# Moving the SBUF addresses of a matmul's two operands against each other in a single-core encoder layer

## The chip, the cores and the metric

The kernel runs on one core of one Trainium2 chip. The metric is the device time of one execution in microseconds (us). It took 939.85 us, the median of 3 runs (939.79 to 940.05).

## The reference, cut to what matters

One layer of an encoder on 512 tokens of width 1024, all in float32:

```
proj   = rms_norm(x) @ w_in                       # 1024 x 4608: xa, zu, zv, gate_a, gate_b
merged = sig(gate_a) * (s5(xa) @ w_proj_a) + sig(gate_b) * (sgu(zu, zv) @ w_proj_b)
h = x + merged @ w_out
h = h + softmax(q k^T / 16) v @ w_xo              # q from h, k and v from 256 memory rows, 4 heads
h = h + (silu(n @ w_gate) * (n @ w_up)) @ w_down  # n = rms_norm(h), 1024 x 2816 x 1024
out = rms_norm(h)
```

`s5` is a bidirectional state-space scan, `sgu` a gating with a 128x128 position matrix per head.

## The kernel before

**A product in three matmuls.** Every operand of a big product is split in two tiles of type float32r, `hi` (a ScalarE copy, L85) and `lo` (VectorE, source minus hi, L86). `mm3` (L264) and `product` (L1203) then issue three matmuls: hi·hi, hi·lo, lo·hi. TensorE holds one 128x128 piece of an operand, the stationary one, and streams 256 or 512 columns of the other, the moving one. Every matmul loads its own stationary piece, and does so while the matmul before it streams.

**Two shapes.** `feat` and `product` hold the weights and stream the tokens. `tokm` holds the tokens and streams 512 columns of weights. The 512-column products are all of `tokm` and `feat` without `n` or `parts`. The 256-column products are:

- the units of `w_gate` and `w_up` (loop at L1260): 10 units of 7 products of 24 matmuls, in Strassen's manner, on quarters of the tokens. In each unit four products stream quarters of `fn` (960 matmuls in all), and three stream sums of quarters kept in `s1`, `s2`, `s4` (720 matmuls);
- `w_k` on the memory rows `mn` (192), the attention scores with `qq` held and `kt` streamed (96), the first head's `w_q` on halves of `hn` (96), the first columns of `w_gate` on halves of `fn`, half of that with the weights in `s1` and `s2` (96), and the last token block of `w_down` (24).

**Weights.** A plan (`plan_block`, `plan_unit`) lists every block of weights in order of use: a load into `raw` from SP's DMA queue, then the split into one of three `whi` and three `wlo` buffers. Weights run a few blocks ahead of TensorE. The order of instructions on each engine is fixed when the program is built.

**Where the tiles lie.** Pools are laid one behind the other in each partition's memory, in the order in which they are opened, and tiles in a pool by tag, each rounded up to 32 bytes. `const` comes first, then `weights` (raw, hi, lo), `slots` (tags A to E of 16 KB each), `norm`, and then the pool of the stage: `s5`, then `merge`, then `xs` with `attn`, then `xs` with `ffn` and `units`. `const` ends 32 bytes past a multiple of 64, so that the weights and all slots start at remainder 288 by 512, and the small tiles of `norm` leave the stages' pools at remainder 96. All sizes inside are multiples of 512 bytes, so one remainder holds for every slice that a matmul reads. `sums_place` (L110) gives one tile of hi and lo for `s1`, `s2`, `s4`. These hold sums of token quarters in the units, weights of a few blocks at the stages' borders (`place=`), and in `w_down` the activations that `split_act` (L195) makes. `xn`, `hn` and `fn`, the tokens after the three norms, lie with hi in slot B and lo in slot C.

Of the kernel before, what the change touches and what calls it, by code (L numbers as in the profile page):

```python
# [9 lines left out]
F32 = mybir.dt.float32  # L10
F32R = mybir.dt.float32r
# [6 lines left out]
P = 128  # L18
D = 1024
T = 512  # L20
NT = T // P
KD = D // P
# [5 lines left out]
C = 16  # L28
GW = 1024
H = 8  # L30
# [22 lines left out]
def hybrid_layer_kernel(  # L53
# [8 lines left out]
    nc = tc.nc  # L62
# [5 lines left out]
    cp = ctx.enter_context(tc.tile_pool(name="const", bufs=1))  # L68
    wp = ctx.enter_context(tc.tile_pool(name="weights", bufs=3))
    sp = ctx.enter_context(tc.tile_pool(name="slots", bufs=1))  # L70
    np_ = ctx.enter_context(tc.tile_pool(name="norm", bufs=2))
# [11 lines left out]
    def split(dst_hi, dst_lo, src, lo_eng=None):  # L83

        nc.scalar.copy(dst_hi, src)  # L85
        (lo_eng or nc.vector).tensor_tensor(dst_lo, src, dst_hi.bitcast(F32), ALU.subtract)  # L86
# [10 lines left out]
    def halves(src, j=None, place=None):  # L97
        _, k, n = src.shape
        if place is None:
            hi = wp.tile([P, k, n], F32R, tag="hi", name="whi", bufs=3)  # L100
            lo = wp.tile([P, k, n], F32R, tag="lo", name="wlo", bufs=3)
        else:
            hl = sums_place(place, k, n)
            hi, lo = hl[:, 0], hl[:, 1]
        split(hi, lo, src, nc.gpsimd if j is not None and j < 2 else None)
        return hi, lo

    sums_pool = [None]

    def sums_place(i, k, n):  # L110
        return sums_pool[0].tile([P, 2, k, n], F32R, tag=f"s{i}", name=f"s{i}", bufs=1)

    def plan_block(w, kb, k, c0, n, more=None, place=None):
        j, got = len(plan), {}
# [80 lines left out]
    def split_act(kb, kpt):  # L195

        hl = sums_place((1, 2, 4)[kb // kpt % 3], kpt, T)
        split(hl[:, 0], hl[:, 1], acts(kb, kpt))
        for k in range(kpt):
            act_hl[kb + k] = (hl[:, 0, k, :], hl[:, 1, k, :])  # L200
# [57 lines left out]
    def load_raw(j):  # L258
        begin(j, j)
# [121 lines left out]
    make_identity(nc, ident)  # L381
    ones = cp.tile([P, P], F32, name="ones")
    nc.vector.memset(ones, 1.0)
    mhalf = cp.tile([P, 1], F32, name="mhalf")
    nc.vector.memset(mhalf, -0.5)

    def sum_sq(dst, src):
# [36 lines left out]
    xsp = [None]  # L424
# [6 lines left out]
    def slot(tag, shape, dt, name):  # L431
        return sp.tile(list(shape), dt, tag=tag, name=name)


    s5 = ExitStack()
    s5p = s5.enter_context(tc.tile_pool(name="s5", bufs=1))
# [9 lines left out]
    for t in range(NT):  # L446
# [4 lines left out]
            load_raw(0)  # L451
        elif t < 3:
            load_raw(t)
    xn_hi = slot("B", (P, KD, T), F32R, "xn_hi")
    xn_lo = slot("C", (P, KD, T), F32R, "xn_lo")
    xn = (xn_hi, xn_lo)
    for t in range(NT):
        rms_scale(xt[:, t, :], g_mix, xt[:, t, :])
# [402 lines left out]
        nc.scalar.activation(z, z, AF.Copy, scale=r)  # L861

    nc.sync.dma_start(wsr, sgu_w[0].rearrange("h t s -> t h s"))
    gbr = np_.tile([2 * H, P], F32, tag="gbr", name="gbr", bufs=1)
    nc.sync.dma_start(gbr[0:H, :], sgu_ln_g[0].rearrange("(h d) -> h d", d=P))
    nc.sync.dma_start(gbr[H:2 * H, :], sgu_ln_b[0].rearrange("(h d) -> h d", d=P))
    mix = np_.tile([P, H, P], F32, tag="gain", name="mix", bufs=2)
# [75 lines left out]
    s5.close()  # L943
    mgx = ExitStack()
    mgp = mgx.enter_context(tc.tile_pool(name="merge", bufs=1))


    yg_hi = mgp.tile([P, 4, T], F32R, name="yg_hi")
# [37 lines left out]

    at = ExitStack()
    xsp[0] = ctx.enter_context(tc.tile_pool(name="xs", bufs=2))
    ap_ = at.enter_context(tc.tile_pool(name="attn", bufs=1))

    h = slot("A", (P, NT, D), F32, "h")
    for t in range(NT):
        nc.sync.dma_start(h[:, t, :], x[t * P:(t + 1) * P, :])
    hn_hi = slot("B", (P, KD, T), F32R, "hn_hi")
    hn_lo = slot("C", (P, KD, T), F32R, "hn_lo")
    hn = (hn_hi, hn_lo)

    mn_hi = ap_.tile([P, KD, M], F32R, tag="mq", name="mn_hi", bufs=2)
# [36 lines left out]


    mn = (mn_hi, mn_lo)
    kt_hi = ap_.tile([P, KD, M], F32R, name="kt_hi")
    kt_lo = ap_.tile([P, KD, M], F32R, name="kt_lo")
    vt_hi = ap_.tile([P, NM, D], F32R, name="vt_hi")  # L1040
# [79 lines left out]

    g_f = gain(ffn_norm_g[0], "g_f")
    ot = (ot_hi, ot_lo)
    fn_hi = slot("B", (P, KD, T), F32R, "fn_hi")
    fn_lo = slot("C", (P, KD, T), F32R, "fn_lo")
    fn = (fn_hi, fn_lo)

    tokm(w_xo, 0, ot, KD, add_evac(0, 1, None), hook=lambda: values(XH - 1, *pts.pop()))
# [52 lines left out]
    a11, a12, a21, a22 = full[:, K0, T0], full[:, K1, T0], full[:, K0, T1], full[:, K1, T1]  # L1180

    def make_op(q, i, src):
        hl = sums_place(i, 4, 256)
        ops[q] = (hl[:, 0], hl[:, 1])
        split(*ops[q], src)

    def sum1():
        V.tensor_tensor(a22, a21, a22, ALU.subtract)
        make_op(5, 1, a22)

    def sum2():
        V.tensor_tensor(s3, a11, a21, ALU.subtract)
        V.tensor_tensor(a11, a22, a11, ALU.subtract)
        make_op(6, 2, a11)

    def sum4():
        V.tensor_tensor(a12, a12, a11, ALU.add)
        make_op(3, 4, a12)
# [176 lines left out]
```

## Time and profile before

| | |
|---|---|
| Median of the runs | 939.85 us |
| The profiled execution, its own time | 940.4 us |
| Its span, first to last instruction | 938.6 us |
| Granted TensorE clock, mean | 0.997 |
| VectorE busy | 577.9 us (62%) |
| ScalarE busy | 442.2 us (47%) |
| GpSimd busy | 84.9 us (9%) |

The chain of work that ended last runs 86% of the span on TensorE. A matmul's duration in the profile is from its start to the modelled end of its last column, so that neighbours overlap. What tells the pace is the distance from one matmul's start to the next one's; a view in order of time gives the starts. "x2" in such a row stands for two equal instructions one behind the other.

### The profile page before, as it was taken

How to read it: one execution, taken by the hardware profiler on the slowest of the kernel's cores; microseconds unless marked ns; L12 is line 12 of the kernel's file. 1: busy time of each engine (PE TensorE's matmuls, PEld its weight loads, DVE VectorE, ACT ScalarE, POOL GpSimd, SP SyncE). 2: the span in 40 equal slices, each digit the busy share in tenths (PEclk: the TensorE clock that was granted, in tenths of full speed). 3: DMA queues.
4: the chain of work that ended last, by engine and by line, in shares of the span. 5: the costliest groups of instructions: out<-in, count | busy, mean ns of one | idle time of the engine just before them, and what ended most of it. 6: DMA issues, size and time to landing. Idle time of an engine off the chain costs nothing.

```text
span 938.6 us, 14044 instructions
## 1 busy us (share of the span) xinstructions
PE 922.0 (98%) x5579; PEld 808.0 (86%) x5579; DVE 577.9 (62%) x943; ACT 442.2 (47%) x643; POOL 84.9 (9%) x136
## 2 busy tenths in 40 slices
PE   7999999999999999999999999999999999999997
PEld 6878888888888888789888888999999999888785
DVE  5696653898462167667545455867667777545544
ACT  5532984244554343545444344644545445433433
POOL 3004210000052104110000001000000000000000
PEclk9999999999999999999999999999999999999999
DMA  8445223323243363735522156244545651222212
GB/s 282 136 135 148 66 91 100 114 90 108 72 115 100 90 204 110 246 91 184 186 80 68 46 174 163 68 112 121 150 116 143 137 122 46 90 90 90 90 67 90
DMA packets 93249, 111.04 MB, mean 118 GB/s; under 512 B 12144, under 2 KB 72064, under 8 KB 93184
## 3 DMA queue, kind: packets, MB, share of 16 engines
q1 hardware_dynamic: 82688, 99.95, 34.4%
q0 software_dynamic: 7328, 7.84, 5.0%
q10 hardware_dynamic: 3168, 2.36, 0.8%
q8 instruction: 44, 0.72, 0.3%
q14 instruction: 21, 0.17, 0.0%
HBM read 103.34 MB, written 6.78 MB: 117 GB/s over the span
## 4 chain that ended last, share of the span: by engine, by line
PE 86%; ACT 5%; DVE 4%; DMA 3%; issue 2%; POOL 1%; SPq 0%; POOLq 0%; DVEq 0%; ACTq 0%
PE pf L267 31%; PE pt L267 24%; PE px L1212 12%; PE pq L1212 6%; PE pv L1212 3%; PE pk L662 1%; DMA b<-in_w_gate_dram 1%; PE po L267 1%; PE psc L267 1%; DMA wraw<-in_w_in_dram 1%; ACT whi L85 1%; PE ptr L419 1%; DVE wlo L86 1%; PE psv L910 1%; PE py L770 1%
## 5 line engine op out<-in xcount | busy, mean ns | idle before, releaser
L86 DVE TENSOR_TENSOR wlo<-wraw,whi 128x1024 fp32r<-128x1024 f32 x110 | 136.9, 1246 | 122.6 <-ACT whi L85 115.2
L85 ACT CAST whi<-wraw 128x1024 fp32r<-128x1024 f32 x112 | 117.6, 1051 | 146.5 <-PE pf L267 82.9
L267 PE MATMUL pt<-whi,s 128*128 128x512 f32 x344 | 107.3, 394 | 1.0 <-ACT whi L85 1.0
L267 PE MATMUL pf<-xn_lo,whi 128*128 128x512 f32 x224 | 88.0, 393 | 0.0
L267 PE MATMUL pf<-xn_hi,whi 128*128 128x512 f32 x224 | 87.9, 393 | 0.0
L267 PE MATMUL pf<-xn_hi,wlo 128*128 128x512 f32 x224 | 87.6, 391 | 0.0
L267 PEld LDWEIGHTS pt<-whi,s 128*128 128x128 f32 x344 | 64.3, 187 | 17.0 <-ACT whi L85 1.2
L86 DVE TENSOR_TENSOR wlo<-b,whi 128x1024 fp32r<-128x1024 f32 x40 | 49.0, 1224 | 36.7 <-ACT whi L85 36.7
L85 ACT CAST whi<-b 128x1024 fp32r<-128x1024 f32 x40 | 42.0, 1051 | 62.3 <-PE px L1212 28.6
L1212 PE MATMUL px<-fn_hi,whi 128*128 128x256 f32 x240 | 68.0, 283 | 1.5 <-ACT u L1270 1.5
L1212 PE MATMUL px<-fn_lo,whi 128*128 128x256 f32 x240 | 68.0, 283 | 0.0
L1212 PE MATMUL px<-fn_hi,wlo 128*128 128x256 f32 x240 | 67.9, 283 | 0.0
L267 PE MATMUL pt<-wlo,s 128*128 128x512 f32 x172 | 67.0, 394 | 0.0
L1212 PE MATMUL pq<-s,whi 128*128 128x256 f32 x320 | 57.1, 280 | 0.0
L86 DVE TENSOR_TENSOR s<-a,s 128x1024 fp32r<-128x1024 f32 x22 | 26.9, 1225 | 48.6 <-ACT s L85 48.6
L267 PEld LDWEIGHTS pf<-xn_hi,whi 128*128 128x128 f32 x224 | 42.1, 188 | 8.8 <-issue 0.2
L267 PEld LDWEIGHTS pf<-xn_hi,wlo 128*128 128x128 f32 x224 | 42.1, 188 | 8.6
L267 PEld LDWEIGHTS pf<-xn_lo,whi 128*128 128x128 f32 x224 | 42.1, 188 | 8.4
L1212 PEld LDWEIGHTS pq<-s,whi 128*128 128x128 f32 x320 | 49.1, 188 | 0.2
L85 ACT CAST s<-a 128x1024 fp32r<-128x1024 f32 x22 | 23.0, 1047 | 54.7 <-PE pt L267 54.7
L86 DVE TENSOR_TENSOR wlo<-t,whi 128x1024 fp32r<-128x1024 f32 x30 | 36.7, 1224 | 18.5 <-ACT whi L85 18.5
L1212 PEld LDWEIGHTS px<-fn_hi,whi 128*128 128x128 f32 x240 | 46.0, 192 | 1.8 <-ACT u L1270 1.8
(352 smaller groups left out, 2316.6 us busy)
## 6 DMA issues: line engine op xcount, KB each, us to landing
wraw<-in_w_in_dram SPq DMA_DIRECT2D x36, 512.0 KB, 3.8
wraw<-in_w_down_dram SPq DMA_DIRECT2D x22, 512.0 KB, 3.6
b<-in_w_gate_dram SPq DMA_DIRECT2D x15, 512.0 KB, 3.9
b<-in_w_up_dram SPq DMA_DIRECT2D x15, 512.0 KB, 4.2
wraw<-in_w_proj_b_dram SPq DMA_DIRECT2D x8, 512.0 KB, 3.7
wraw<-in_w_out_dram SPq DMA_DIRECT2D x8, 512.0 KB, 4.4
wraw<-in_w_k_dram SPq DMA_DIRECT2D x8, 512.0 KB, 4.6
wraw<-in_w_v_dram SPq DMA_DIRECT2D x8, 512.0 KB, 3.6
```

The costliest lines, as they stand in the source:

```text
L85: nc.scalar.copy(dst_hi, src)
L86: (lo_eng or nc.vector).tensor_tensor(dst_lo, src, dst_hi.bitcast(F32), ALU.subtract)
L267: nc.tensor.matmul(ps, a[x], b[y], start=start and i == 0, stop=stop and i == 2, skip_group_check=free)
L419: nc.tensor.transpose(ps[:, j, :], src[:, k * P:(k + 1) * P], ident)
L662: nc.tensor.matmul(ps[32 * j:32 * j + 32, q, :], bd[i][:, g].rearrange("p d c -> p (d c)"), lc(es[i], g), start=(i == 0), stop=False, tile ...
L770: nc.tensor.matmul(ps[:, g, :], tt[:, g, :], u[:, o * GO + g, :], start=True, stop=False)
L910: nc.tensor.matmul(ps[:, t * P:(t + 1) * P], zt[:, t, h * P:(h + 1) * P], wst[:, h, :], start=True, stop=True)
L1212: nc.tensor.matmul(ps[:, j, :], a[x], b[y], start=start and j == k == i == 0, stop=k == 3 and i == 2, skip_group_check=True)
```

## The change

It changes addresses. What each engine computes stays: the instructions of TensorE, ScalarE and VectorE are the same in the same order. Three small clears on GpSimd are new, and two loads stand elsewhere in SP's queue.

- `mhalf` takes 36 bytes instead of 4, which moves all that lies behind it by 32.
- `xn`, `hn` and `fn` become one tile of hi and lo in tag B, with 512 bytes to spare; `fn` starts 64 bytes in. Tag C goes.
- `sums_place` has 512 bytes to spare too, and an argument `shift`: the sums of token quarters start 320 bytes in; weights and activations placed there start at 0.
- Pads of 192 bytes at the start of `merge` and of `xs`, and one of 64 bytes, `shift`, ahead of `kt` and `vt`; each is cleared once.
- `gbr`, which had a tag of its own, takes a buffer of tag "gain".

Start addresses by 512, in the built programs (the difference is moving minus stationary, by 512):

| products | moving, stationary before | difference | after | difference |
|---|---|---|---|---|
| 512 columns, weights with xn, hn, yb, mg, ot | 288, 288 | 0 | 320, 320 | 0 |
| 512 columns, `w_down` and `w_v` | 288, 96 | 192 | 320, 320 | 0 |
| 512 columns, yg, ya, part of `w_xo` | 96, 288 | 320 | 320, 320 | 0 |
| 512 columns, first `w_up` block on fn | 288, 288 | 0 | 384, 320 | 64 |
| 512 columns, attention values | 96, 96 | 0 | 384, 384 | 0 |
| 256 columns, units on fn | 288, 288 | 0 | 384, 320 | 64 |
| 256 columns, units on sums | 96, 288 | 320 | 128, 320 | 320 |
| 256 columns, scores | 96, 96 | 0 | 384, 320 | 64 |
| 256 columns, `w_k` on mn | 96, 288 | 320 | 320, 320 | 0 |
| 256 columns, first head's `w_q` | 288, 288 | 0 | 320, 320 | 0 |
| 256 columns, fn with weights in s1, s2 | 288, 96 | 192 | 384, 320 | 64 |
| 256 columns, last block of `w_down` | 288, 96 | 192 | 320, 320 | 0 |

All starts before are 32 past a multiple of 64; all starts after are multiples of 64.

```diff
-    def sums_place(i, k, n):
-        return sums_pool[0].tile([P, 2, k, n], F32R, tag=f"s{i}", name=f"s{i}", bufs=1)
+    def sums_place(i, k, n, shift=0):
+        t = sums_pool[0].tile([P, 2 * k * n + 128], F32R, tag=f"s{i}", name=f"s{i}", bufs=1)
+        return t[:, shift:shift + 2 * k * n].rearrange("p (h k n) -> p h k n", h=2, k=k)
+
+    def align(pool):
+
+        pad = pool.tile([P, 48], F32, name="pad", bufs=1)
+        nc.gpsimd.memset(pad, 0.0)
...
-    mhalf = cp.tile([P, 1], F32, name="mhalf")
+    mhalf = cp.tile([P, 9], F32, name="mhalf")[:, 0:1]
...
+    def token_slot(name, shift=0):
+
+        t = sp.tile([P, 2 * KD * T + 128], F32R, tag="B", name=name)
+        hl = t[:, shift:shift + 2 * KD * T].rearrange("p (h k t) -> p h k t", h=2, k=KD)
+        return hl[:, 0], hl[:, 1]
...
-    xn_hi = slot("B", (P, KD, T), F32R, "xn_hi")
-    xn_lo = slot("C", (P, KD, T), F32R, "xn_lo")
+    xn_hi, xn_lo = token_slot("xn")
...
-    gbr = np_.tile([2 * H, P], F32, tag="gbr", name="gbr", bufs=1)
+    gbr = np_.tile([2 * H, P], F32, tag="gain", name="gbr", bufs=2)
...
     mgp = mgx.enter_context(tc.tile_pool(name="merge", bufs=1))
+    align(mgp)
...
     xsp[0] = ctx.enter_context(tc.tile_pool(name="xs", bufs=2))
+    align(xsp[0])
...
-    hn_hi = slot("B", (P, KD, T), F32R, "hn_hi")
-    hn_lo = slot("C", (P, KD, T), F32R, "hn_lo")
+    hn_hi, hn_lo = token_slot("hn")
...
+    shift = ap_.tile([P, 16], F32, name="shift")
+    nc.gpsimd.memset(shift, 0.0)
     kt_hi = ap_.tile([P, KD, M], F32R, name="kt_hi")
...
-    fn_hi = slot("B", (P, KD, T), F32R, "fn_hi")
-    fn_lo = slot("C", (P, KD, T), F32R, "fn_lo")
+    fn_hi, fn_lo = token_slot("fn", 16)
...
-        hl = sums_place(i, 4, 256)
+        hl = sums_place(i, 4, 256, 80)
```

## The prediction

> **What bounds the kernel now.** I first read the page's busy times and its granted clock.
>
> ```profile
> PE 922.0 (98%) x5579; PEld 808.0 (86%) x5579; DVE 577.9 (62%) x943; ACT 442.2 (47%) x643; POOL 84.9 (9%) x136
> PEclk9999999999999999999999999999999999999999
> ```
>
> TensorE is never long without a matmul and its clock is full. Then busy times by stage (columns: window, length, busy and instruction count of PE, PEld, DVE, ACT, POOL, then clock, DMA share, GB/s):
>
> ```profile
> 90.00:175.00 85.00, 84.00 (x496) 72.64 (x495) 49.22 (x108) 58.81 (x88) 10.29 (x21) 1.00 0.31 97
> 580.00:810.00 230.00, 227.34 (x1852) 224.22 (x1852) 167.43 (x169) 116.80 (x147) 11.37 (x10) 1.00 0.44 109
> 810.00:932.00 122.00, 121.72 (x536) 97.91 (x535) 59.81 (x66) 46.99 (x59) 1.66 (x3) 1.00 0.25 86
> ```
>
> In the units VectorE, the next busiest, works 167.4 of 230 us. So the time is the number of matmuls times their spacing, and the change can act only through the spacing. The view in order of time gives it: the first and the last start of a stretch, divided by the matmuls from one to the other. Here are five address cases: fn in a unit, a sum in a unit, xn, `w_down`, yg; and below them `w_k` and the program's last matmuls.
>
> ```profile
> 637.05 0.29 PE L1212 MATMUL px<-fn_hi,wlo 128*128 128x256 f32 x1
> ...
> 639.93 0.28 PE L1212 MATMUL px<-fn_hi,wlo 128*128 128x256 f32 x1
> ```
> ```profile
> 634.21 0.28 PE L1212 MATMUL px<-s,wlo 128*128 128x256 f32 x1
> ...
> 636.33 0.28 PE L1212 MATMUL px<-s,wlo 128*128 128x256 f32 x1
> ```
> ```profile
> 180.10 0.39 PE L267 MATMUL pf<-xn_hi,whi 128*128 128x512 f32 x1
> ...
> 186.90 0.39 PE L267 MATMUL pf<-xn_hi,whi 128*128 128x512 f32 x1
> ```
> ```profile
> 816.36 0.39 PE L267 MATMUL pt<-wlo,s 128*128 128x512 f32 x1
> ...
> 824.76 0.39 PE L267 MATMUL pt<-wlo,s 128*128 128x512 f32 x1
> ```
> ```profile
> 340.45 0.39 PE L267 MATMUL pf<-yg_hi,whi 128*128 128x512 f32 x1
> ...
> 346.63 0.39 PE L267 MATMUL pf<-yg_hi,whi 128*128 128x512 f32 x1
> ```
> ```profile
> 426.04 0.28 PE L267 MATMUL pf<-mn_hi,wlo 128*128 128x256 f32 x1
> ...
> 427.06 0.28 PE L267 MATMUL pf<-mn_hi,wlo 128*128 128x256 f32 x1
> ```
> ```profile
> 929.29 0.28 PE L267 MATMUL pcut<-wlo,s 128*128 128x256 f32 x1
> ...
> 931.34 0.28 PE L267 MATMUL pcut<-wlo,s 128*128 128x256 f32 x1
> ```
>
> The same element comes back every third matmul, so the counts are multiples of three. Spacing: fn 2.88 us / 24 = 120.0 ns; sums 2.12 / 18 = 117.8; xn 6.80 / 30 = 226.7; `w_down` 8.40 / 36 = 233.3; yg 6.18 / 27 = 228.9; `w_k` here 1.02 / 9 = 113.3; the last ones 2.05 / 18 = 113.9.
>
> Two things are to be seen. **Equal work has unequal spacing by address**: 512 columns take 226.7 ns at difference 0, 228.9 at 320, 233.3 at 192. And **the spacings come in steps**: 256 more columns at difference 0 cost 226.7 - 120.0 = 106.7 ns for 1024 bytes, while 120.0 - 113.3 and 233.3 - 226.7 are both 6.67 ns, a sixteenth of 106.7. So a step is 64 bytes of the moving operand, and in steps the spacings are 17, 17 2/3 and 18 for 256 columns, whose data fill 16, and 34, 34 1/3 and 35 for 512 columns, whose data fill 32. Nothing falls below 17. I read that as reads in 64-byte blocks: 1024 bytes that start 32 past a multiple of 64 touch 17 blocks, 2048 touch 33, and the rest (nothing to two steps) is lost to the weight load beside them, by the difference of the addresses.
>
> **The change part by part.** TensorE, VectorE and ScalarE issue the same instructions, so the sum has one kind of term: a class's matmuls times its change of spacing. Counts are from the loops.
>
> *All starts become multiples of 64.* If the first step is the straddled block, each of the 4620 float32r matmuls loses 6.67 ns: 30.8 us. The trace of before shows no float32r operand at a multiple of 64, so this is bounded: nothing, if the seventeenth step is a fixed gap between matmuls, or one step. I take one step, as 113.3 is the floor in two classes and is exactly 17 blocks.
>
> *Differences.* Where rows show a case, I keep what it loses beyond the first step: one step at 0, and 2/3 of a step at 320 with 256 columns. A difference of 64 isn't shown; its nearest row is 320 with sums, the other odd number of blocks near it: 2/3 of a step, 111.1 ns when aligned. Bounds: no loss (106.7) and two steps as in `w_down` (120.0).
>
> | class | matmuls | before, ns | after, ns | us |
> |---|---|---|---|---|
> | fn in units, scores | 1056 | 120.0 | 111.1 | -9.4 |
> | sums in units | 720 | 117.8 | 111.1 | -4.8 |
> | 512 columns at 0, stays | 1536 | 226.7 | 220.0 | -10.2 |
> | `w_down`, `w_v`: 192 to 0 | 612 | 233.3 | 220.0 | -8.2 |
> | yg, ya, `w_xo`: 320 to 0 | 192 | 228.9 | 220.0 | -1.7 |
> | first head's `w_q` | 96 | 120.0 | 113.3 | -0.6 |
> | `w_k`, fn with s1/s2, last block, `w_up`'s first, values | 408 | | | -1.7 |
>
> The last row is a rest of small classes, estimated from the same steps. Sum: -36.6 us.
>
> A rule of the Trainium skill ("TensorE: Matmul & The Clock Gate", section "Back-to-back issue gap") gives a warm spacing of columns / 2.4 + 2.5 ns, so 109.2 and 215.8 here. The rows lie above it throughout, 113.3 at the least. If all classes came down to it, the estimated sum would be -52 us and the time 888.
>
> *What doesn't become time.* Up to 175 us VectorE feeds the scan and the order is fixed, so a faster TensorE meets some waits earlier. About 480 float32r matmuls lie there, 3.2 us by one step; I count half, +1.6. Later VectorE has room: 167.4 us in a units stage that shrinks from 230 to about 215.
>
> *The rest of the edits.* Three clears of 192 bytes or less on GpSimd and a moved `g_mem` load:
>
> ```profile
> 358.73 3.52 POOL L979 TENSOR_TENSOR mg<-mg,part 128x512 f32<-128x512 f32 x2 [50.21 <-issue]
> ```
> ```profile
> 141.01 8.46 SPq L118 DMA_DIRECT2D wraw<-in_w_in_dram  x2
> 151.66 9.26 SPq L895 DMA_DIRECT2D gad<-gas  x2
> ```
> ```profile
> 148.21 0.23 PE L877 MATMUL pgb<-ident,gbr 16*128 16x16 f32 x1
> ```
>
> GpSimd idles 50 us before the merge's first addition, which covers the first pad; without that cover it would cost a fraction of a microsecond there. `g_mem` now shares `gbr`'s buffer, so its load stands in SP's queue between the two weight loads of the 141 us row and waits for the transpose at 148.2. The second of them is issued by 149.5 at the latest (the row's end), so one SP issue may slip by about 1 us, with weights running two blocks ahead: nothing. `mix` waits for the last read of `g_mix` early on: nothing. Uncovered, both together would cost 1 to 2 us.
>
> Sum: 940.4 - 36.6 + 1.6 = 905.4 for the profiled execution; it ran 0.55 over the median, so **905 us**.
>
> **The rivals.**
>
> *Alignment does nothing, differences do* (the seventeenth step is a fixed gap). For: no row shows an aligned operand. Against: a fixed gap needn't be exactly one block long. Then fn and scores gain 2.2 ns x 1056 = 2.3 us, `w_down` and `w_v` 6.67 x 612 = 4.1, yg 0.4; `w_k` goes from 320 to 0 and loses about 0.6, small classes 0.4. Net -5.8: 934.
>
> *Alignment helps one of the shapes alone*, because with 256 columns the weight load fills nearly the whole spacing (PEld 224.2 of 230 us in the units) and with 512 it doesn't (97.9 of 122). Only 512 columns: -20.6 - 1.7 = -22; only 256: -16 - 4.5 = -20. About 919.
>
> *Slower.* At difference 64 the moving operand runs one block ahead of the weights, as `w_down`'s runs three ahead at 192, and loses a step more than level instead of a third less: 126.7 ns on 1056 matmuls, +7.0 us. Without an alignment gain, `w_down` gives back 4.1 and `w_k` and small ones take 0.7: 943 or so. It decides if 64 costs more than 124 ns in the units. Against: sums at 320 and `w_k` are below level.
>
> *Nothing changes.* The spacing could hang on what is held and streamed and not on addresses: `w_down` streams weights, the units stream tokens. Then 940. Against it are the two spacings of `feat` alone, 226.7 on xn and 228.9 on yg, and the 120.0 and 117.8 of one line, L1212. The Trainium skill ("SBUF — State Buffer", section "Who interferes with whom") says that TensorE reads the moving operand and the weights through two independent ports and never waits for anyone, by which no address could matter; these four rows disagree.
>
> **How the numbers follow.** Forecast 0.50; differences alone 0.24; one shape alone 0.13; slower 0.08; nothing 0.05. The forecast's own range is 897 to 913: half a step more or less on the 2340 matmuls of 512 columns in the table is 7.8 us. The range that leaves out no more than 2 in 10 must take in one shape alone and differences alone with fn at its bounds: 898 to 937. Faster by over 0.2% (about what a measurement of this kernel can tell from no change) 0.87, within 0.05, slower 0.08.
>
> **What would show it.** In the profile after: xn's spacing 220 against 226.7 decides on alignment; `w_down` must equal xn (if it stays at 233, the address difference isn't its cause); fn in the units at 111 and sums at 111 as well; `w_k` no more than 113.3. Busy VectorE and ScalarE stay at 578 and 442 us. A wait on `wraw` near 150 us, or a longer gap in TensorE before 175 us, would show the cost of what I left at nothing. It is wrong if xn stays at 226.7, or if fn rises above 120.

## The result and the profile after

The changed kernel took 929.79 us (median of 6 runs, 928.02 to 935.31) against 939.84 for the kernel before on the same chip: a ratio of 0.989, 95% interval [0.9857, 0.9923]. The forecast was 905 us. The sign was right, the size less than a third of what was said. Two later series of the changed kernel gave 931.07 us (0.9906, [0.9879, 0.9932]) and 935.68 us (0.9937, [0.9912, 0.9962]). Why one kernel has these medians is a part of the answer below.

The profiled execution after took 929.58 us, with a span of 927.8. The page's busy times and granted clock:

```profile
PE 910.8 (98%) x5579; PEld 801.7 (86%) x5579; DVE 577.3 (62%) x943; ACT 442.3 (48%) x643; POOL 85.0 (9%) x139
PEclk9999999999999999999999999999999999999999
```

TensorE still bounds the kernel, with the same 5579 matmuls; VectorE and ScalarE are busy as before. So the difference lies in the spacing, and the view in order of time gives it again: fn in a unit, sums in a unit, xn, `w_down`, `w_k` (line numbers have moved: L1225 is `product`, L273 `mm3`).

```profile
637.17 0.28 PE L1225 MATMUL px<-fn,wlo 128*128 128x256 f32 x1
...
639.89 0.28 PE L1225 MATMUL px<-fn,wlo 128*128 128x256 f32 x1
```
```profile
628.78 0.39 PE L1225 MATMUL pq<-s,whi 128*128 128x256 f32 x2
...
631.16 0.39 PE L1225 MATMUL pq<-s,whi 128*128 128x256 f32 x2
```
```profile
179.99 0.39 PE L273 MATMUL pf<-xn,wlo 128*128 128x512 f32 x1
...
186.79 0.39 PE L273 MATMUL pf<-xn,wlo 128*128 128x512 f32 x1
```
```profile
816.10 0.39 PE L273 MATMUL pt<-wlo,s 128*128 128x512 f32 x1
...
824.26 0.39 PE L273 MATMUL pt<-wlo,s 128*128 128x512 f32 x1
```
```profile
428.14 0.28 PE L273 MATMUL pf<-mn_hi,wlo 128*128 128x256 f32 x1
...
430.30 0.28 PE L273 MATMUL pf<-mn_hi,wlo 128*128 128x256 f32 x1
```

Spacing: fn 2.72 us / 24 = 113.3 ns (before 120.0); sums 2.38 / 21 = 113.3 (117.8); xn 6.80 / 30 = 226.7 (226.7); `w_down` 8.16 / 36 = 226.7 (233.3); `w_k` 2.16 / 18 = 120.0 (before 113.3 in part and 117.8 in the rest). The decisive row is xn: every start is a multiple of 64 now, and not a nanosecond has gone.

By stages: from the first unit's product on sums to the first `w_down` matmul took 191.50 us before and 182.62 after, from there to the start of the last matmul 128.81 and 125.66. Up to the units the changed kernel is 1.32 us later. That sums to -10.7; the spans differ by 10.8. The 1.32 come from a stretch at half clock, which cost 1.6 us, less 0.3 won on the way, and not from an edit. Windows before, then after (length, busy of PE, PEld, DVE, ACT, POOL, granted clock, DMA share, GB/s):

```profile
10.00:15.00 5.00, 3.58 (x10) 2.49 (x11) 3.96 (x5) 4.14 (x11) 4.20 (x3) 0.66 1.04 346
30.00:40.00 10.00, 10.00 (x52) 7.98 (x50) 5.63 (x18) 6.62 (x9) 0.00 (x0) 1.00 0.46 123
```
```profile
10.00:15.00 5.00, 2.65 (x11) 1.73 (x11) 4.06 (x5) 4.50 (x12) 4.20 (x3) 1.00 1.03 339
30.00:40.00 10.00, 10.00 (x45) 7.86 (x44) 5.03 (x16) 6.01 (x8) 0.00 (x0) 0.83 0.34 100
```

Both executions lose 1.7 us' worth of clock, (1 - 0.66) x 5 and (1 - 0.83) x 10: once while TensorE waits for the first loads (busy 3.58 of 5 us), where it costs nothing, and once under full work, where it costs 1.6 us. The Trainium skill ("TensorE: Matmul & The Clock Gate", section "What's actually happening") says that the clock is set by a free-running window of about 3.4 us, so that the place of a change varies from run to run; with that these rows agree. The Trainium skill there puts half clock behind an idle window, which they don't show: in the changed kernel TensorE is busy for all of the 4 us from 30 to 34, and the clock is half from 34 on.

### The profile page after: what moved, and what is told of

The parts are those of the page before. It is cut to its first block, busy times and chain, and to the rows that moved or that the text cites. A ratio compares the mean times of both kernels' runs of the same rounds, so it can differ in the third digit from the quotient of the medians.

```text
span 927.8 us, 14051 instructions
## 1 busy us (share of the span) xinstructions
PE 910.8 (98%) x5579; PEld 801.7 (86%) x5579; DVE 577.3 (62%) x943; ACT 442.3 (48%) x643; POOL 85.0 (9%) x139
## 4 chain that ended last, share of the span: by engine, by line
PE 85%; ACT 5%; DVE 4%; DMA 3%; issue 2%; POOL 1%; SPq 0%; POOLq 0%; ACTq 0%; DVEq 0%
PE pf L273 31%; PE pt L273 24%; PE px L1225 11%; PE pq L1225 6%; PE pv L1225 3%; PE pk L673 1%; DMA b<-in_w_gate_dram 1%; PE po L273 1%; ACT whi L85 1%; PE psc L273 1%; DVE wlo L86 1%; DMA wraw<-in_w_in_dram 1%; PE ptr L425 1%; PE psv L921 1%; PE py L781 1%
## 5 line engine op out<-in xcount | busy, mean ns | idle before, releaser
L273 PE MATMUL pf<-xn,whi 128*128 128x512 f32 x448 | 141.0, 393 | 0.0
L273 PE MATMUL pt<-whi,s 128*128 128x512 f32 x344 | 105.4, 390 | 1.0 <-ACT whi L85 1.0
L273 PEld LDWEIGHTS pf<-xn,whi 128*128 128x128 f32 x448 | 83.7, 188 | 17.2 <-issue 0.2
L273 PE MATMUL pf<-xn,wlo 128*128 128x512 f32 x224 | 87.6, 391 | 0.0
L1225 PE MATMUL px<-fn,whi 128*128 128x256 f32 x480 | 83.9, 277 | 1.6 <-ACT u L1283 1.6
L273 PEld LDWEIGHTS pt<-whi,s 128*128 128x128 f32 x344 | 64.5, 188 | 14.7 <-ACT whi L85 1.2
L1225 PEld LDWEIGHTS px<-fn,whi 128*128 128x128 f32 x480 | 72.6, 188 | 1.8 <-ACT u L1283 1.7
L1225 PE MATMUL px<-fn,wlo 128*128 128x256 f32 x240 | 66.4, 277 | 0.0
L273 PE MATMUL pt<-wlo,s 128*128 128x512 f32 x172 | 66.2, 390 | 0.0
L1225 PE MATMUL pq<-s,whi 128*128 128x256 f32 x320 | 55.1, 276 | 0.0
L273 PEld LDWEIGHTS pf<-xn,wlo 128*128 128x128 f32 x224 | 42.1, 188 | 8.5
L1225 PEld LDWEIGHTS pq<-s,whi 128*128 128x128 f32 x320 | 48.3, 188 | 0.2
L85 ACT CAST whi<-t 128x1024 fp32r<-128x1024 f32 x30 | 31.6, 1054 | 31.9 <-PE pv L1225 11.3
L273 PE MATMUL pt<-whi,xn 128*128 128x512 f32 x128 | 43.3, 411 | 2.0 <-ACT xn L85 1.7
L1225 PEld LDWEIGHTS px<-fn,wlo 128*128 128x128 f32 x240 | 45.1, 188 | 0.0
```

The source lines that it names most:

```text
L273: nc.tensor.matmul(ps, a[x], b[y], start=start and i == 0, stop=stop and i == 2, skip_group_check=free)
L1225: nc.tensor.matmul(ps[:, j, :], a[x], b[y], start=start and j == k == i == 0, stop=k == 3 and i == 2, skip_group_check=True)
```

## The experiments

Theory first: only the difference of the two addresses counts. Rival: the forecast's blocks, where alignment takes a step off each matmul.

**e1_off64**: the changed kernel with everything 32 past a multiple of 64 again, same differences.

```diff
-    mhalf = cp.tile([P, 9], F32, name="mhalf")[:, 0:1]
+    mhalf = cp.tile([P, 1], F32, name="mhalf")
```

> The changed kernel with mhalf back at 4 bytes: every address behind it moves by 32, so all starts are 32 past a multiple of 64 again and every difference stays that of the changed kernel. Theory D (differences alone count): as the changed kernel, 929.8 us, units at 113.3 ns on fn and on sums. Theory A (the sums came down from 117.8 to 113.3 because of the multiples of 64): units at 117.8 ns throughout, 4.5 ns x 1680 = 7.5 us more, 937.

Measured 935.47 us (927.16 to 940.13, 9 runs), 0.9913 [0.9878, 0.9948]; the profiled execution 927.16. xn and fn in its view in order of time:

```profile
179.88 0.39 PE L273 MATMUL pf<-xn,wlo 128*128 128x512 f32 x1
...
182.60 0.39 PE L273 MATMUL pf<-xn,wlo 128*128 128x512 f32 x1
...
641.54 0.28 PE L1225 MATMUL pv<-fn,wlo 128*128 128x256 f32 x1
...
642.22 0.28 PE L1225 MATMUL pv<-fn,wlo 128*128 128x256 f32 x1
```

2.72 / 12 = 226.7 and 0.68 / 6 = 113.3: as aligned. Its nine runs lie at 927.2 to 927.4 (four) and 935.5 to 940.1 (five); of that below. Its half-clock stretch lay where that of before lies, and its span is 925.4, 13.2 below before, where the 10.8 of the changed kernel and the 1.6 us that the stretch didn't cost here make 12.4.

**e2_align**: the kernel before, aligned, all differences kept (the diff of e1_off64 turned round).

> The kernel before with mhalf at 36 bytes: all starts multiples of 64, every difference as before. Theory D: as before, 939.8 us, fn 120.0, sums 117.8, w_down 233.3 ns. Theory A: sums at 113.3 ns, 4.4 x 720 = 3.2 us less, 936.6.

Measured 940.65 us, 0.9997 [0.9984, 1.001].

```profile
180.27 0.39 PE L267 MATMUL pf<-xn_hi,wlo 128*128 128x512 f32 x1
...
182.31 0.39 PE L267 MATMUL pf<-xn_hi,wlo 128*128 128x512 f32 x1
...
636.89 0.28 PE L1212 MATMUL px<-fn_hi,wlo 128*128 128x256 f32 x1
...
638.33 0.28 PE L1212 MATMUL px<-fn_hi,wlo 128*128 128x256 f32 x1
```

2.04 / 9 = 226.7 and 1.44 / 12 = 120.0. Alignment to 64 does nothing, alone or with the rest.

**e3_fn**: of the change, only fn at 64; sums stay at 320, `w_down` at 192.

```diff
-    fn_hi = slot("B", (P, KD, T), F32R, "fn_hi")
-    fn_lo = slot("C", (P, KD, T), F32R, "fn_lo")
+    fn_hi, fn_lo = token_slot("fn", 16)
```

(`xn`, `hn` by `token_slot` too, unshifted, and `gbr` in tag "gain", for the room.)

> The kernel before with fn alone moved by 64 bytes (xn, hn, fn in one tile, gbr in tag gain, nothing else): in the units fn at difference 64, sums still at 320, all 32 past a multiple of 64. Theory D with history (a product at 0 puts the next ones at 113.3's slower neighbour 117.8, products at 64 and 320 hold 113.3): both at 113.3, 6.4 + 3.2 = 9.6 us less, 930. Theory A: fn and sums 117.8, 2.1 us less, 937.7.

Measured 931.44 us (930.93 to 933.66), 0.9904 [0.9888, 0.992]. The sums, whose addresses it doesn't touch:

```profile
628.31 0.39 PE L1216 MATMUL pq<-s,whi 128*128 128x256 f32 x2
...
630.69 0.39 PE L1216 MATMUL pq<-s,whi 128*128 128x256 f32 x2
```

2.38 / 21 = 113.3 in place of 117.8. So a product's pace is not its own alone: the products before it seem to count. This is one profile, and the pace turns out below to vary by execution; but all five runs lie within 3 us, and no run of the kernel before comes down to where sums at 113.3 would put it.

**e4_down**: only `w_down`'s operands level, in the kernel before.

```diff
-    def sums_place(i, k, n):
+    def sums_place(i, k, n, shift=48):
...
-        hl = sums_place(i, 4, 256)
+        hl = sums_place(i, 4, 256, 0)
```

> The kernel before with weights and activations in s1, s2, s4 moved level with the other weights, sums where they were: w_down from difference 192 to 0. Both theories: w_down 226.7 instead of 233.3 ns, 3.4 us less, and 0.3 us back in the first columns of w_gate; 936.7. If w_down stays at 233.3 it is its roles and not its addresses.

Measured 938.85 us, 0.997 [0.9957, 0.9982].

```profile
820.13 0.39 PE L268 MATMUL pt<-wlo,s 128*128 128x512 f32 x1
...
822.85 0.39 PE L268 MATMUL pt<-wlo,s 128*128 128x512 f32 x1
```

2.72 / 12 = 226.7: this part of the change is worth what it says, 3 us.

**f1_128, f2_192, f3_256, f4_32**: fn, sums, xn and hn moved together to another distance from the weights, in search of a pace below the floor. The edit, with n = 32, 48, 64 elements of four bytes:

```diff
-    xn_hi, xn_lo = token_slot("xn")
+    xn_hi, xn_lo = token_slot("xn", n)
...
-    hn_hi, hn_lo = token_slot("hn")
+    hn_hi, hn_lo = token_slot("hn", n)
...
-    fn_hi, fn_lo = token_slot("fn", 16)
+    fn_hi, fn_lo = token_slot("fn", n)
...
-        hl = sums_place(i, 4, 256, 80)
+        hl = sums_place(i, 4, 256, n)
```

(f4_32: 8 for fn and sums, 4 for xn and hn.)

> The changed kernel with fn, the sums, xn and hn all 128 bytes past the weights' remainder. So far 256 columns took 120.0 ns at differences 0 and 256, and 113.3 or 117.8 at 64, 192 and 320. Theory P (an odd number of 64-byte blocks between the two streams is good, an even one is bad): 256 columns 120.0 ns, as level; about 940 us. Theory N (only nearness to level or to 256 is bad): 113.3 or 117.8. For 512 columns on xn, P gives 226.7 as at 0.

> The same with 192 bytes. Theory P: units at 113.3 ns as with 64 and 320, 226.7 there no more: 512 columns on xn at 228.9 (as 64 and 320, tokens streamed) to 233.3 (192 in w_down, weights streamed), about 5 us more than the changed kernel, 935. If 64 and 320 are special, the units stay at 117.8 or above.

> The same with 256 bytes. Theory P and the 120.0 ns seen on fn at 256 with weights in s1 and s2: units at 120.0, xn at 226.7 as level; about 940 us.

> The changed kernel with fn and the sums 32 bytes past the weights' remainder, xn and hn 16 bytes past. If blocks of 64 bytes count, 32 and 16 bytes are still the same block for half the stream or more: 117.8 to 120.0 ns for 256 columns, 226.7 for 512. If a smaller block counts, 32 bytes are one block or more and the units come to 113.3, or under it.

One run each: 941.78, 933.79, 938.41, 937.38 us. xn in f1_128, f2_192 and f3_256:

```profile
180.33 0.39 PE L273 MATMUL pf<-xn,wlo 128*128 128x512 f32 x1
...
182.42 0.40 PE L273 MATMUL pf<-xn,wlo 128*128 128x512 f32 x1
```
```profile
180.66 0.39 PE L273 MATMUL pf<-xn,wlo 128*128 128x512 f32 x1
...
183.46 0.39 PE L273 MATMUL pf<-xn,wlo 128*128 128x512 f32 x1
```
```profile
180.01 0.39 PE L273 MATMUL pf<-xn,wlo 128*128 128x512 f32 x1
...
182.05 0.39 PE L273 MATMUL pf<-xn,wlo 128*128 128x512 f32 x1
```

2.09 / 9 = 232.2; 2.80 / 12 = 233.3; 2.04 / 9 = 226.7. With the units' spacings, over all traces:

| difference by 256 | 512 columns, ns | 256 columns, ns |
|---|---|---|
| 0 | 226.7 | 120.0 |
| 16 | 231.7 | 119 |
| 32 | 233 | 117 |
| 64 | 229 | 113.3 or 117.8 |
| 128 | 232 | 119 to 120 |
| 192 | 233.3 | 113.3, at places 117.8 |

256 is like 0, and 320 like 64: so far as these two pairs show it, the period is 256 bytes. The figures are those of settled stretches: the attention values, level in every version but in runs of a dozen matmuls at most, took 230 to 231 ns. The two widths want opposite things, level for 512 and not level for 256. Nothing fell below 113.3 and 226.7.

**g3_cut and h1_cut64: what the floor is.** Every level 512-column matmul of some stages is cut in two over the same weights.

```diff
+        c = width[0] if ps.shape[-1] == 512 else None
         for i, (x, y) in enumerate(((0, 0), (0, 1), (1, 0))):
+            if c:
+                nc.tensor.matmul(ps[:, :c], a[x], b[y][:, :c], start=start and i == 0, stop=stop and i == 2, skip_group_check=True)
+                nc.tensor.matmul(ps[:, c:], a[x], b[y][:, c:], start=False, stop=stop and i == 2, skip_group_check=True)
+                continue
```

> The changed kernel with every 512-column matmul on the stages' normed tokens, attention and w_down cut in two over the same weights, all level: 384 and 128 columns on xn and yb, 320 and 192 on hn and mn, 256 and 256 on ot and in w_down. Theory of a fixed gap: a level matmul takes its columns at 106.67 ns per 256 and 13.33 ns beside them (120.0 and 226.7 fit that), so 384 columns take 173.3, 320 take 146.7, 128 take 66.7 if no weight load holds them, 256 take 120.0; about 2000 cuts cost 13.3 ns each, 27 us, some 956 us. Rival: the columns themselves go one seventeenth slower than 16 columns in 6.67 ns, and what lies above is the difference's: then 384 take 170.0, 320 take 141.7, and only the halves of w_down and ot cost 13 ns (the level 120.0), 9 us, some 939. A weight load longer than a short piece would show as a pace above both for 128 and 192 columns.

> The changed kernel with 512-column matmuls cut in two over the same weights, level, at other widths: 448 and 64 columns on xn and yb, 352 and 160 on hn and mn; ot, w_down and the first w_up block stay whole. The cuts of 384 and 128 took 286.7 ns a pair, 60.0 over the whole, and those of 320 and 192 took 257.5; a fixed gap alone says 240. Theory of a floor: a matmul's columns take 106.67 ns per 256 and 13.3 beside them, but no matmul is shorter than the load of the weights that follow it, about 113.3. Then 448 and 64 take 186.7 + 13.3 + 113.3 = 313.3 a pair, 352 and 160 take 146.7 + 13.3 + 113.3 = 273.3. Rival: the dearer pairs come from the cut itself (the same weights loaded twice, the second piece's start within the row), not from the short piece's length; then a pair costs 286.7 or 257.5 at these widths too. Units, with the first w_up block whole, at 113.3 by the theory that this block sets their pace; at 117.8 if it was anything else in the cuts of before.

Measured 1015.83 and 1060.3 us, one run each. The first is far above both expectations, 956 and 939; the theory of a floor was made from its spacings, and h1_cut64 tests it at other widths. (h1_cut64's granted clock was 0.76 from 20 to 120 us; its spacings are taken from behind that.) Pairs of 384 and 128 on xn in g3_cut; of 448 and 64 on xn, and 352 and 160 on hn, in h1_cut64:

```profile
181.32 0.39 PE L277 MATMUL pf<-xn,wlo 128*128 128x384 f32 x1
181.54 0.22 PE L278 MATMUL pf<-xn,wlo 128*128 128x128 f32 x1
...
183.90 0.39 PE L277 MATMUL pf<-xn,wlo 128*128 128x384 f32 x1
```
```profile
300.38 0.45 PE L277 MATMUL pf<-xn,wlo 128*128 128x448 f32 x1
300.67 0.19 PE L278 MATMUL pf<-xn,wlo 128*128 128x64 f32 x1
...
302.26 0.45 PE L277 MATMUL pf<-xn,wlo 128*128 128x448 f32 x1
...
624.44 0.36 PE L277 MATMUL pf<-hn,wlo 128*128 128x352 f32 x1
...
627.68 0.36 PE L277 MATMUL pf<-hn,wlo 128*128 128x352 f32 x1
```

A pair takes 2.58 / 9 = 286.7, 1.88 / 6 = 313.3 and 3.24 / 12 = 270.0 ns; 320 and 192 took 257.5 in g3_cut, and two level halves of 256 took 2 x 120.0. A fixed gap says 240 for all of them, a gap in proportion to the columns 227, a price of the cut itself one number for all. Columns at 106.7 per 256, 13.3 beside them, and **no matmul that takes less than some 110 to 113 ns** say 283 to 287, 310 to 313, 270 to 273 and 257 to 260. (So taken, 128 and 64 columns came out at 113.3, 192 at 110.8 and 160 at 110.0.) Only whole pairs can be read so: inside a pair the starts lie 0.22 and 0.06 us apart, so the wait shows behind the long piece's start. The rows of the weight loads (PEld) of g3_cut tell why a pair is long:

```profile
181.26 0.19 PEld L277 LDWEIGHTS pf<-xn,wlo 128*128 128x128 f32 x1
181.37 0.19 PEld L278 LDWEIGHTS pf<-xn,wlo 128*128 128x128 f32 x1
181.55 0.19 PEld L277 LDWEIGHTS pf<-xn,whi 128*128 128x128 f32 x1
```

The load for a long piece starts when the short one before it starts (181.54 and 181.55), and the next load comes 0.11 us behind it; over all the cut stages of both kernels, never less than 107 ns behind. The kernel before has the floor too, without a cut, in matmuls of the scan and of the gating on plain float32:

```profile
140.06 1.89 PE L719 MATMUL pz<-u,wt 128*128 128x64 f32 x16
169.81 1.84 PE L910 MATMUL psv<-wsx,zt 128*128 128x128 f32 x15
```

But for the first one, the starts of both lie 111 to 112 ns apart, with 64 columns as with 128, and every one loads 128x128 weights. So 113.3 is the least that a 256-column matmul with a new 128x128 load took: a floor that doesn't go with the columns, and no block. That it is the load itself fits all these rows, but no run changed the load. The Trainium skill ("TensorE: Matmul & The Clock Gate", section "LDWEIGHTS (loading the stationary operand)") gives a load of 128 columns 128 / 1.2 = 107 ns; the 0.11 us from load to load agree, and the floor of the spacing is 3 to 7 ns above that.

**g1_sums0, c_after, h2_up256: the two paces.** g1_sums0 puts the sums level, fn stays at 64; h2_up256 cuts the first `w_up` block in halves (`width[0] = 256` around that one `feat`); c_after is the changed kernel again.

```diff
-        hl = sums_place(i, 4, 256, 80)
+        hl = sums_place(i, 4, 256)
```

> The changed kernel with the sums of token quarters placed level with the weights (difference 0), fn still at 64. Theory of two paces: at differences 64 and 320 a 256-column product runs at 113.3 or at 117.8 ns, whichever the matmuls before it left behind, and a level product between them leaves 117.8. Then fn in the units runs at 117.8 here and the sums at 120.0; against the changed kernel that is 960 x 4.4 ns + 720 x 6.7 ns = 9 us more, some 938 us. Rival: each product has the pace of its own difference and 64 has 113.3. Then fn stays at 113.3, the sums go to 120.0, and it is 4.8 us more, some 934.

> The changed kernel with one edit: the first w_up block on fn (48 matmuls of 512 columns at difference 64) is cut in halves of 256 columns. Theory that the pace is left behind by the matmuls before: the 256-column products ahead of it run at 117.8 and nothing of 512 columns comes between, so the whole units, 1680 matmuls with unchanged addresses and unchanged instructions, run at 117.8 in place of 113.3: 7.5 us more, some 938 us. Rival: the units' pace comes from their own addresses; then they stay at 113.3 and the time within 0.5 us of the changed kernel's.

> The changed kernel once more, on the same chip as the others of this call, for the comparison: some 930 us against 940 by every theory.

Measured 936.29 (one run), 942.15 (one run, at half clock from 580 to 587 us) and 931.07 us (927.52 to 936.51). In g1_sums0 fn ran at 117.8 and the sums at 120.0, in h2_up256 everything in the units ran at 117.8, both as the theory of paces said. But so did the units in c_after's profiled execution (935.3 us), where nothing was changed: its units took 189.55 us against 182.62. So h2_up256 shows nothing of its own, and g1_sums0 only that level sums take 120.0. And in h1_cut64, where the `w_up` block was whole, they ran at 117.8: that this block sets the pace has fallen.

**g2_best, k_192, c_after2.** g2_best: fn and sums at 192, and mn at 64. k_192: fn and sums at 192 alone. c_after2: the changed kernel a third time, beside k_192.

```diff
-    fn_hi, fn_lo = token_slot("fn", 16)
+    fn_hi, fn_lo = token_slot("fn", 48)
...
-        hl = sums_place(i, 4, 256, 80)
+        hl = sums_place(i, 4, 256, 48)
```

> The changed kernel with fn and the sums at 192 in place of 64 and 320, and mn at 64 (one more pad of 64 bytes ahead of it, which puts w_v's operands 64 the other way). Theory of two paces: at 192 the 256-column products ran at 113.3 all the way, so the 195 that run at 117.8 in the changed kernel gain 0.9 us, the first w_up block loses 48 x 4.5 ns = 0.2, w_k goes from 120.0 to 113.3 or 117.8 and gains 0.4 to 1.3 us, w_v stays or gains 0.1: 1.1 to 2.1 us below the changed kernel, some 928. Rival: the pace of 192 hung on xn and hn being at 192 too; then it is level with the changed kernel or a little above.

> The changed kernel with fn and the sums at 192 in place of 64 and 320, and nothing else. At 64 and 320 the units ran at 113.3 ns in the first profile of the changed kernel and at 117.8 in the second, 7.5 us apart over 1680 matmuls, and its times fall in two groups, 928 to 931 and 935 to 937. Theory that 192 fixes the pace: at 192 the units ran at 113.3 in both profiles there are, so the median is some 929 (0.9 us for the products ahead of the units, which run at 117.8 at 64, less 0.2 us for the first w_up block) and no run lies above 933. Rival: 192 has both paces too, by execution; then some third of the runs lie at 935 to 938 here as well.

> The changed kernel a third time, on the chip of the run beside it, for the count of the two groups: by the theory of a pace chosen anew in each execution, some runs at 927 to 931 and some, a third or so, at 935 to 937; by the rival that the second profile was a disturbance, all at 927 to 931.

g2_best: 929.92 us (927.86 to 932.83), 0.9876 [0.9856, 0.9896], not told apart from c_after beside it. mn at 64 gave `w_k` 117.8, but `w_v`, 64 the other way, 233.3 in place of 226.7, a loss where none was expected. k_192: 928.50 us (927.60 to 929.44), 0.9869 [0.9852, 0.9885], the fastest version and the steadiest; c_after2 935.68 (927.58 to 936.86). fn in a unit of c_after2 and of k_192:

```profile
641.65 0.28 PE L1225 MATMUL px<-fn,wlo 128*128 128x256 f32 x1
...
643.77 0.28 PE L1225 MATMUL px<-fn,wlo 128*128 128x256 f32 x1
```
```profile
637.26 0.28 PE L1225 MATMUL px<-fn,wlo 128*128 128x256 f32 x1
...
639.98 0.28 PE L1225 MATMUL px<-fn,wlo 128*128 128x256 f32 x1
```

2.12 / 18 = 117.8 and 2.72 / 24 = 113.3. The changed kernel's 19 runs in the three series fall in two groups, ten from 927.5 to 931.5 and nine from 934.3 to 936.9; the profiled ones show why: the units take 182.6 or 189.6 us, by execution.

## Why the prediction was wrong

**The step that failed** is "All starts become multiples of 64": "I take one step, as 113.3 is the floor in two classes and is exactly 17 blocks." Nothing was to be had; this step carried 30.8 of the 36.6 us. Two facts had been put into one: 113.3 at 256 columns is the floor of a matmul with a new load, and 226.7 at 512, level, is 32 steps of columns and 13.3 ns beside them. That both are multiples of 17 is chance by this reading. The level rows shown before the result already held the other reading, 120.0 = 106.7 + 13.3 and 226.7 = 213.3 + 13.3. A block touched by misalignment would have added one step to either width, not one to 256 and two to 512. And the scan's 64-column matmuls, whose data fill 4 blocks and not 16, lay at 112 ns in the trace before.

Term by term, in us, for the two paces of the units (the profiled executions of after and c_after2):

| term | forecast | units at 113.3 | at 117.8 |
|---|---|---|---|
| fn and sums in the units | -14.2, with the scores | -8.9 | -2.0 |
| 512 columns at 0, stays | -10.2 | 0 | 0 |
| `w_down`, `w_v` | -8.2 | -3.7 | -3.7 |
| yg, ya, `w_xo` | -1.7 | -0.4 | -0.4 |
| `w_q` and small classes | -2.3 | +0.6 (the rest) | +0.7 (the rest) |
| waits before 175 us | +1.6 | 0 | 0 |
| half clock under work | none | +1.6 | +1.9 |
| span | -35.0 | -10.8 | -3.5 |

**The differences** were right where a row showed them: `w_down` equals xn, shown by e4_down alone, and 192 to 0 is worth 6.67 ns on 612 matmuls. 64, which no row showed, was taken from 320, and that nearest row was right (64 and 320 are the same). But the rows had 320 in two paces, and the forecast took them for two things: the sums' 117.8 for the price of 320, and the 113.3 of `w_k`, also at 320, for the floor of all. In the same trace most of `w_k` ran at the sums' pace (132 of its 192 matmuls at 117 to 119 ns, 51 at 113 or 114):

```profile
416.93 0.28 PE L267 MATMUL pf<-mn_hi,wlo 128*128 128x256 f32 x1
...
417.99 0.28 PE L267 MATMUL pf<-mn_hi,wlo 128*128 128x256 f32 x1
```

1.06 / 9 = 117.8, 9 us ahead of the stretch at 113.3. In the units of the kernel before, a level fn product stands between the sums, and they ran at 117.8; e3_fn shows that they run at 113.3 where fn isn't level. (With sums at 113.3 the kernel before would take 720 x 4.4 ns = 3.2 us less, 936.6; none of its runs is below 938.7.)

**The rival "differences alone"** was what happened, at 0.24. Its 934 us is the changed kernel in the slower pace (934.3 to 936.9); that a faster pace existed for fn and the sums, it missed.

**"Nothing changes"** had two grounds: what is held and what is streamed, and the Trainium skill's "SBUF — State Buffer", section "Who interferes with whom", with two ports that never wait. e4_down and f1_128 to f4_32 disagree: same operations, same order, 226.7 to 233.3 by the address difference alone. The 109.2 and 215.8 by the rule of the Trainium skill ("TensorE: Matmul & The Clock Gate", section "Back-to-back issue gap"), which it gives for an isolated matmul, weren't reached at any address that was tried.

**Hidden edits**: the pads, `g_mem`'s place in SP's queue and `mix` cost nothing that can be seen. From 45 us, behind the half-clock stretch, to 330 us, the two executions keep their distance within 0.2 us. The waits that I expected before 175 us had no cause, since TensorE there became no faster; +1.6 came from another thing by coincidence.

**Open**: what decides between 113.3 and 117.8. The pace is taken up at a border and kept through up to 1600 matmuls; in the profile after it goes from 113.3 to 117.8, at the same addresses, at an idle stretch of 1.55 us near 790 us. In three traces whose units ran at 113.3 (after, e1_off64, e3_fn) the first spacing of the `w_up` block is 235 ns, in three at 117.8 (c_after, c_after2, h1_cut64) it is 229, one step less: a phase between two streams would look so, but that is argued only. (g1_sums0 began with 235 too, and its fn ran at 117.8 behind level sums.) Whether 192 can fall into the slower pace for a whole stage is open too; in the units of three profiles it did so only near 800 us, for some 30 to 50 matmuls in each, and none of k_192's five runs lies in the upper group; but f2_192's `w_q`, 96 matmuls at 192, ran at 117.8 throughout. How the two addresses act on each other inside TensorE, no run shows.

## What to carry to other kernels

With a new weight load per matmul, the spacing depends on the address difference of the two operands by 256 bytes: 512 columns want 0, 256 columns don't; here that was worth 0.6 to 1.3%, by the pace that was met. A common shift of both operands was tried by 32 bytes only, and did nothing. Before a step in a spacing is read as a cause, fit it over two widths, and test it by moving one number. When a time comes in two groups, profile the same kernel twice before explaining a difference between two kernels.

## What the runs showed of the hardware that was not expected

- One program, one set of addresses, two paces of TensorE: 113.3 or 117.8 ns for over 1500 matmuls, by execution, 6.9 us on the units.
- Period 256 bytes; 16 and 32 bytes off level already cost 512 columns 5 to 7 ns.
- Behind a longer one, a 128-column or 64-column matmul with a new load costs as much as one of 256 columns at its best, 113.3 ns; 64-column and 128-column float32 ones in a row cost 112.
- A stretch at half clock lay in the first 40 us of 17 of the 18 profiled executions (in g3_cut the first came at 645 us); one of 3.4 us cost 0 or 1.6 us by what it fell on.
